# Odd experts choose their body by a row of conditional blocks, with prefetch hints for the skips at the head of each body

## The chip, the cores and the metric

One core of a Trainium2 chip runs one program. The metric is device time in microseconds (us): the median of the runs, beside one execution that the hardware profiler recorded. TensorE is called PE, VectorE DVE, ScalarE ACT and SyncE SP; SP issues the DMAs.

## What is computed

A two-layer trunk over 256 latent and 256 context tokens of width 1024. Layer 0 is a convolution and gating mixer with a dense SwiGLU. Layer 1 is a latent attention followed by a top-2-of-8 expert SwiGLU, and the change lies in the experts:

```python
def _moe(h, router, w1, w3, w2):
    ...
    logits = (hf @ router).astype(jnp.float32)
    top_v, top_i = lax.top_k(logits, TOP_K)             # TOP_K = 2 of 8
    top_w = jax.nn.softmax(top_v, axis=-1)
    gates = jnp.sum(jax.nn.one_hot(top_i, N_EXPERTS, dtype=jnp.float32) * top_w[..., None], axis=-2).astype(h.dtype)
    for e in range(N_EXPERTS):                           # D_EXPERT = 3584
        y = y + gates[:, e:e + 1] * _swiglu(hf, w1[e], w3[e], w2[e])
```

## The kernel before

Everything ahead of the experts is straight code. The router's result says how many of the 256 tokens chose each expert. The program rounds that up to groups of 32 tokens and packs, for all eight experts, a two-bit class into one integer `packed` (`class_of`, L1094). Class 0 means one group, 1 two groups, 2 three groups, 3 four groups. Each engine loads `packed` into a register (L1330) and branches on it by itself.

`expert(e, s)` (L1183) is the body of expert `e` for `s` groups. It streams the expert's weights, 42 pieces of 1 MB, through a ring of 21 rooms in SBUF; SP issues the load of a later piece as soon as PE has given a room back (`ring.load`, L172). In the body, `up` (L1198) multiplies by the first two weight matrices, `turn` (L1214) transposes, `down` (L1227) multiplies by the third, `spread` (L1253) and `scatter` (L1274) put the result back to its tokens, and DVE adds it to the stream (L1278). All f32 matmuls of `up`, `down` and `scatter` become four PE instructions each, two weight loads and two matmuls. Ahead of every even expert `gather` (L1128) collects the tokens of two experts.

For each expert four bodies stand in the program, for three, one, four and two groups, and one of them runs. Before the change they are nested else-branches (L1349 to L1358): the outermost condition is `groups != 2`, and the body for three groups is its Else. A block that ends with its Else lies last, so in the program's layout the order is one, four, two, three groups, and then the code that follows, which is called the join here. Whoever leaves the body for one, four or two groups jumps over the rest to the join; whoever leaves the body for three groups is there.

`tc.mark_branch_hint_location` puts a BRANCH_PREFETCH_HINT for a named branch into PE's program: it tells PE's instruction fetch where that branch will probably go. Without an expression it says that the branch jumps away from the block that follows it; with an expression a register decides. Before the change the named branches are the outermost ones alone, one for each expert. The order of PE, ACT and DVE is written out by hand (`ordered()`, L1109).

In the profiled execution the experts 0 to 7 have 3, 1, 4, 3, 3, 1, 3 and 3 groups.

Of the kernel before, what the change touches and what calls it, by code (L numbers as in the profile page):

```python
# [33 lines left out]
N_EXP = 8  # L34
# [210 lines left out]
def trunk(ctx: ExitStack, tc, w, out, taps=None):  # L245
# [19 lines left out]
    def scratch(dtype=F32):  # L265
        return tmp.tile([P, T], dtype, tag="tmp", name="scratch")
# [230 lines left out]
    with tc.tile_pool(name="mix", bufs=1, side="right", reuse_waits="tile") as mix:  # L497
# [163 lines left out]
        for m in range(4):  # L661
# [6 lines left out]
            s = scratch()  # L668
# [81 lines left out]
    with tc.tile_pool(name="ffn", bufs=1, side="right", reuse_waits="tile") as fp:  # L750
# [12 lines left out]
        for t in range(3):  # L763
            f0, f1 = FF_CUT[t], FF_CUT[t + 1]
            f = f0
            if t == 0:
# [5 lines left out]
                f = 2  # L772
            for f in range(f, f1):
                a1 = one(f"f1_{f}", hi, lo, T)
                a3 = one(f"f3_{f}", hi, lo, T)
                s = act(f - f0, a1, a3)
# [201 lines left out]
    more = right.enter_context(tc.tile_pool(name="more", bufs=1, side="right", reuse_waits="tile"))  # L978
# [52 lines left out]
    As, Bs = [bank("A") for _ in range(4)], [bank("B") for _ in range(2)]  # L1031
# [24 lines left out]
    other = lg.unsqueeze(2).to_broadcast([P, 2, N_EXP, N_EXP])  # L1056
# [52 lines left out]
    def ordered():  # L1109
        return tc.manual_schedule(engines={mybir.EngineType.PE, mybir.EngineType.Activation, mybir.EngineType.DVE})  # L1110

    with tc.tile_pool(name="exp", bufs=1, side="right", reuse_waits="tile") as ep:
# [219 lines left out]

        fg_row = xf_all[:, :, 0, :]

        def announce(e):
            tc.mark_branch_hint_location(f"groups{e}", hint=(packed // 4**e) % 4 != 2, engines={mybir.EngineType.PE})

        for e in range(N_EXP):
            groups = (packed // 4**e) % 4
            state = ring.loaded, ring.used  # L1340

            def body(s):
                ring.loaded, ring.used = state
                with ordered():
                    if e % 2 == 0:
                        announce(e + 1)
                    expert(e, s)

            with tc.If(groups != 2, preferred_fallthrough_block=True, label=f"groups{e}") as other:  # L1349
                with tc.If(groups == 0, preferred_fallthrough_block=True) as one:  # L1350
                    body(1)
                with one.Else():
                    with tc.If(groups == 3, preferred_fallthrough_block=True) as four:
                        body(4)
                    with four.Else():
                        body(2)
            with other.Else():
                body(3)  # L1358
            if e % 2 and e + 1 < N_EXP:
                with ordered():  # L1360
                    announce(e + 1)
                    gather([Bs[0], As[0], Bs[1], As[1]] * 2)
        assert ring.used == len(ring.pieces) == ring.loaded
        with ordered():
            final_norm()
# [196 lines left out]
```

## Time and profile before

| what | value |
|---|---|
| median of 3 runs | 1695.11 us (1694.89 to 1697.21) |
| the profiled execution's own time | 1693.19 us |
| its span, from the first to the last instruction | 1691.40 us |
| PE busy | 1606.8 us, 95% of the span |
| mean granted clock of PE | 0.982 |
| chain of work that ended last | PE 88%, DMA 6%, DVE 4% |
| PE, idle at the join behind expert 1 / inside expert 2's choice | 5.00 / 5.37 us |
| PE, idle at the join behind expert 2 / behind expert 5 | 8.17 / 5.18 us |

The experts take the last 930 us of the span. The granted clock is the share of PE's full 2.4 GHz that was granted in a stretch: 1.0 or 0.5 (1.2 GHz). In the views, "issue" as the end of an idle time says that the engine waited for nothing that the profile shows as work. PEq and PEldq are PE's sequencer, which reads instructions some time before they run; a COMPARE_BRANCH there is a branch, and its duration is the time until the next instruction could be read. Queue q8 of the DMA carries PE's instructions.

### The profile page before, as it was taken

What the parts mean: (1) busy time and instruction counts of PE and PEld (TensorE: products, weight loads), DVE (VectorE), ACT (ScalarE), POOL (GpSimd) and SP (SyncE); (2) the same over time, 40 slices, a digit from 0 to 9 for tenths busy, and PEclk for the clock granted to TensorE, in tenths of its full rate; (3) what the DMA queues carried; (4) which work ended last, traced back from release to release, by engine and by line L of the source; (5) the groups of instructions that cost most, each with busy time, mean ns of one, the idle gap of its engine ahead of it and who ended that gap; (6) DMA issues with size and microseconds to landing.
All of it is one profiled execution on the core that took longest, in us unless ns stands there. A gap on an engine that the chain in (4) does not pass through costs nothing.

```text
span 1691.4 us, 40719 instructions
## 1 busy us (share of the span) xinstructions
PE 1606.8 (95%) x18697; PEld 1100.3 (65%) x18697; DVE 518.3 (31%) x945; ACT 381.6 (23%) x708; POOL 23.1 (1%) x20
## 2 busy tenths in 40 slices
PE   8998999999999999999997699979999996999996
PEld 5776678888888877796553455545565552656554
DVE  4899773333333567751010100010010011001001
ACT  4353452222222355542000000000010010000101
POOL 0013000000000000000000000000000000000000
PEclk9999999999999999999999799989999997999999
DMA  9661663322322355599999999869989999999970
GB/s 383 234 246 54 248 246 100 100 87 95 101 90 84 103 196 209 200 370 383 398 380 420 417 417 387 297 215 383 389 311 382 392 395 419 417 418 418 418 287 28
DMA packets 67322, 470.23 MB, mean 278 GB/s; under 512 B 7456, under 2 KB 7840, under 8 KB 13088
## 3 DMA queue, kind: packets, MB, share of 16 engines
q1 hardware_dynamic: 67104, 467.13, 70.7%
q8 instruction: 160, 2.62, 0.6%
q14 instruction: 58, 0.48, 0.1%
HBM read 466.05 MB, written 1.05 MB: 276 GB/s over the span
## 4 chain that ended last, share of the span: by engine, by line
PE 88%; DMA 6%; DVE 4%; issue 1%; ACT 1%; SPq 0%; DVEq 0%; ACTq 0%
PE bankA L1198 29%; PE bankB L1227 14%; PE bankA L270 7%; PE bankA L271 7%; PE bankA L272 7%; DMA raw<-e 5%; PE bankB L271 3%; PE bankB L270 3%; PE bankB L272 3%; DVE cv L525 2%; PE bankC L340 2%; PE bankC L1214 1%; PE bankA L1274 1%; DMA room<-e 1%; PE bankA L340 1%
## 5 line engine op out<-in xcount | busy, mean ns | idle before, releaser
L1198 PE MATMUL bankA<-room,xf_all 128*32 128x256 f32 x4704 | 265.9, 384 | 14.4 <-issue 8.5
L1208 DVE TENSOR_TENSOR scratch<-scratch,bankA 128x256 f32<-128x256 f32 (+1 forms) x98 | 31.6, 352 | 721.8 <-ACT scratch L1207 721.8
L1198 PEld LDWEIGHTS bankA<-room,xf_all 128*32 128x32 f32 x4704 | 154.3, 111 | 116.4 <-issue 23.2
L1198 PE MATMUL bankA<-raw,xf_all 128*32 128x256 f32 x3024 | 171.6, 382 | 7.4 <-DMA raw<-e 7.3
L132 DVE TENSOR_TENSOR split<-raw,split 128x1024 fp32r<-128x1024 f32 (+4 forms) x121 | 139.9, 1159 | 113.4 <-ACT split L131 111.2
L131 ACT CAST split<-raw 128x1024 fp32r<-128x1024 f32 (+4 forms) x121 | 118.1, 981 | 199.4 <-PE bankA L272 121.2
L1207 ACT ACTIVATE scratch<-bankA 128x256 f32<-128x256 f32 (+1 forms) x98 | 32.5, 331 | 546.5 <-PE bankA L1198 542.8
L270 PE MATMUL bankA<-hq,split 128*128 128x512 f32 (+1 forms) x380 | 149.3, 393 | 1.3 <-ACT hq L451 1.3
L271 PE MATMUL bankA<-hq,split 128*128 128x512 f32 (+1 forms) x380 | 148.2, 390 | 0.9 <-DVE hq L454 0.9
L1227 PE MATMUL bankB<-raw,scratch 128*32 128x256 f32 x2352 | 138.6, 386 | 8.4 <-DMA raw<-e 7.9
L272 PE MATMUL bankA<-hq,split 128*128 128x512 f32 (+1 forms) x380 | 146.4, 385 | 0.0
L1198 PEld LDWEIGHTS bankA<-raw,xf_all 128*32 128x32 f32 x3024 | 96.6, 110 | 74.1 <-DMA raw<-e 9.6
L1227 PEld LDWEIGHTS bankB<-raw,scratch 128*32 128x32 f32 x2352 | 75.9, 111 | 64.0 <-DMA raw<-e 9.4
L1198 PE MATMUL bankA<-roomsplit,xf_all 128*32 128x256 f32 x1680 | 96.3, 384 | 6.0 <-DMA roomsplit<-e 6.0
L525 DVE SCALAR_TENSOR_TENSOR cv<-pad,prm,cv 128x512 f32<-128x512 f32 x106 | 86.0, 848 | 0.8
L270 PEld LDWEIGHTS bankA<-hq,split 128*128 128x128 f32 x380 | 71.6, 189 | 21.9 <-ACT hq L451 3.4
L1198 PEld LDWEIGHTS bankA<-roomsplit,xf_all 128*32 128x32 f32 x1680 | 53.6, 111 | 45.4 <-DMA roomsplit<-e 9.7
L271 PEld LDWEIGHTS bankA<-hq,split 128*128 128x128 f32 x380 | 71.7, 189 | 15.6 <-DVE hq L454 1.4
L272 PEld LDWEIGHTS bankA<-hq,split 128*128 128x128 f32 x380 | 71.5, 188 | 15.4 <-DVE split L132 0.2
L1216 ACT COPY scratch<-bankC 128x384 f32<-128x384 f32 (+2 forms) x56 | 24.6, 440 | 234.3 <-PE bankC L1214 234.3
L1227 PE MATMUL bankB<-room,scratch 128*32 128x256 f32 x1344 | 76.9, 379 | 0.0
L271 PE MATMUL bankB<-hq,split 128*128 128x512 f32 (+1 forms) x172 | 66.9, 389 | 1.4 <-DVE hq L276 1.4
(409 smaller groups left out, 2011.6 us busy)
## 6 DMA issues: line engine op xcount, KB each, us to landing
room<-e SPq DMA_DIRECT2D x144, 1024.0 KB, 10.9
raw<-e SPq DMA_DIRECT2D x125, 1024.0 KB, 12.1
roomsplit<-e SPq DMA_DIRECT2D x63, 1024.0 KB, 14.7
raw<-ada SPq DMA_DIRECT2D x48, 1024.0 KB, 7.9
raw<-f SPq DMA_DIRECT2D x26, 1024.0 KB, 5.1
raw<-f SPq DMA_DIRECT2D x8, 896.0 KB, 4.7
raw<-win SPq DMA_DIRECT2D x6, 1024.0 KB, 8.2
raw<-wout SPq DMA_DIRECT2D x4, 1024.0 KB, 8.3
```

Of the source, the lines that this page charges most:

```text
L131: self.nc.scalar.copy(wh[:, :size], raw)
L132: self.nc.vector.tensor_sub(wl[:, :size], raw, wh[:, :size].bitcast(F32))
L270: nc.tensor.matmul(acc, wh, ah, start=first, stop=False)
L271: nc.tensor.matmul(acc, wh, al, start=False, stop=False)
L272: nc.tensor.matmul(acc, wl, ah, start=False, stop=last)
L340: nc.tensor.matmul(acc[32 * q : 32 * q + 32, :], cs[:, 4 * h + q, :], wt[:, q, :], start=(h == 0), stop=(h == 1), tile_position=(0, 32 * q))
L525: nc.vector.scalar_tensor_tensor(out=o, in0=i, scalar=cw[:, m, j : j + 1], in1=o, op0=ALU.mult, op1=ALU.add)
L1198: nc.tensor.matmul(accs[g // 2][32 * q : 32 * q + 32, g % 2], xf[:, k, g * GROUP : (g + 1) * GROUP], piece[:, k - kk, :, q * P : (q + 1) * ...
L1207: nc.scalar.activation(part, acc[:, :n, 0, :], AF.Silu)
L1208: nc.vector.tensor_mul(part, part, acc[:, :n, 1, :])
L1216: nc.scalar.copy(ht[:, : s * P], tp[:, : s * P])
L1227: nc.tensor.matmul(ys[g // 2][32 * t : 32 * t + 32, g % 2], ht[:, g * P + f * GROUP : g * P + (f + 1) * GROUP], piece[:, f - ff, t, :], st ...
```

## The change

Even experts keep the nested else-branches. For odd experts each body gets a conditional block of its own, one behind the other, in the order three, one, four, two groups, so that there is nothing to jump over from else to else, but whoever leaves a body comes to a condition that is false and skips the rest. At the head of each odd body but the last stands a hint, without an expression, for the skip that follows this body. At the head of each even body stands a hint with an expression for the first branch of the odd expert that follows. Behind an odd expert, ahead of `gather`, two hints are written: for the even expert's outermost branch, as before, and for its branch to the one-group body, which is new.

```diff
-        def announce(e):
-            tc.mark_branch_hint_location(f"groups{e}", hint=(packed // 4**e) % 4 != 2, engines={mybir.EngineType.PE})
+        def hint(label, expr=None):
+            tc.mark_branch_hint_location(label, hint=expr, engines={mybir.EngineType.PE})
+
+        def case(cond, label=None):
+            return tc.If(cond, preferred_fallthrough_block=True, label=label)
 
         for e in range(N_EXP):
             groups = (packed // 4**e) % 4
+            after = (packed // 4 ** (e + 1)) % 4
             state = ring.loaded, ring.used
-
-            def body(s):
+            enter = f"three{e + 1}", after == 2
+
+            def body(s, leave):
                 ring.loaded, ring.used = state
                 with ordered():
-                    if e % 2 == 0:
-                        announce(e + 1)
+                    if leave:
+                        hint(*leave)
                     expert(e, s)
...
+            if e % 2:
+                with case(groups == 2, f"three{e}"):
+                    body(3, [f"other{e}"])
+                with case(groups != 2, f"other{e}"):
+                    with case(groups == 0):
+                        body(1, [f"more{e}"])
+                    with case(groups != 0, f"more{e}"):
+                        with case(groups == 3):
+                            body(4, [f"two{e}"])
+                        with case(groups != 3, f"two{e}"):
+                            body(2, None)
+                if e + 1 < N_EXP:
+                    with ordered():
+                        hint(f"one{e + 1}", (packed // 4 ** (e + 1)) % 2 == 0)
+                        hint(f"groups{e + 1}", after != 2)
+                        gather([Bs[0], As[0], Bs[1], As[1]] * 2)
+            else:
+                with case(groups != 2, f"groups{e}") as other:
+                    with case(groups == 0, f"one{e}") as one:
+                        body(1, enter)
+                    with one.Else():
+                        with case(groups == 3) as four:
+                            body(4, enter)
+                        with four.Else():
+                            body(2, enter)
+                with other.Else():
+                    body(3, enter)
```

Three places in PE's program, as built. The first is the join behind expert 0, where expert 1 begins. In the rows, `L1336 ISA` and `REGISTER_ALU` work out a hint's register, `room` and `raw` are rooms of the ring and `xf_all` is the gathered tokens. Before:

```order
L1349 UNCONDITIONAL_BRANCH
L1336 ISA
L1336 REGISTER_ALU
L1557 BRANCH_PREFETCH_HINT
L1349 REGISTER_ALU x2
L1349 COMPARE_AND_BRANCH
L1350 REGISTER_ALU x2
L1350 COMPARE_AND_BRANCH
L1198 MATMUL bankA<-room_5422,xf_all 32x256 x8
```

After:

```order
L1372 UNCONDITIONAL_BRANCH
L1356 REGISTER_ALU x2
L1356 COMPARE_AND_BRANCH
L1576 BRANCH_PREFETCH_HINT
L1198 MATMUL bankA<-room_5422,xf_all 32x256 x24
```

The hint that stood here (it is that of expert 2's outermost branch, put here by the scheduler, one expert ahead of its branch) is gone, and the three-group body (x24) follows the first branch, with the hint for its own exit at its head.

The second place is the end of expert 1's one-group body. Before, it ends with a jump to the join, and the next condition follows:

```order
L1274 MATMUL bankA<-scratch 128x256
L1274 MATMUL bankC<-scratch 128x256
L1350 UNCONDITIONAL_BRANCH
L1353 REGISTER_ALU x2
L1353 COMPARE_AND_BRANCH
```

After:

```order
L1359 UNCONDITIONAL_BRANCH x2
L1361 COMPARE_AND_BRANCH
L1362 REGISTER_ALU x2
L1362 COMPARE_AND_BRANCH
L1576 BRANCH_PREFETCH_HINT
L1198 MATMUL bankA<-room_5422,xf_all 32x256 x32
```

The jump to the join has become the conditional branch of L1361, to which a hint at the body's head belongs.

The third place is the join behind expert 1, ahead of the gather (`G_all`, `tok_h`) for the experts 2 and 3. Before:

```order
L1274 MATMUL bankA<-scratch 128x256
L1274 MATMUL bankC<-scratch 128x256
L1349 UNCONDITIONAL_BRANCH
L1128 MATMUL bankB<-G_all,tok_h 128x256 x2
L1128 MATMUL bankB<-G_all,tok_l 128x256 x2
```

After:

```order
L1364 UNCONDITIONAL_BRANCH x2
L1361 UNCONDITIONAL_BRANCH
L1358 UNCONDITIONAL_BRANCH
L1336 ISA
L1336 REGISTER_ALU
L1576 BRANCH_PREFETCH_HINT
L1128 MATMUL bankB<-G_all,tok_h 128x256 x2
```

One hint now stands directly ahead of the gather, and it belongs to the outermost branch of the even expert behind that gather. The second hint that the source writes there, for the branch to the one-group body, is not in the built program. The same holds behind the experts 3 and 5.

## Rows read from the trace of the kernel before

**Rows 1.** The page: span, and the DMA queue of instructions (packets, MB, share).

```profile
span 1691.4 us, 40719 instructions
...
q8 instruction: 160, 2.62, 0.6%
```

**Rows 2.** PE's timeline at joins: start us, us, what, count, [idle before, what ended it].

```profile
947.64 0.80 PE L1128 MATMUL bankB<-G_all,tok_h 128*128 128x256 f32 x2 [5.00 <-issue]
...
959.44 6.82 PE L1198 MATMUL bankA<-room,xf_all 128*32 128x256 f32 x88 [5.37 <-DMA room<-e]
...
1125.15 11.04 PE L1198 MATMUL bankA<-room,xf_all 128*32 128x256 f32 x152 [8.17 <-issue]
...
1427.12 0.48 PE L1274 MATMUL bankA<-scratch 32*128 32x256 f32 x2 [0.64 <-DVE scratch L1263]
...
1433.44 0.80 PE L1128 MATMUL bankB<-G_all,tok_h 128*128 128x256 f32 x2 [5.18 <-issue]
...
1439.73 6.63 PE L1198 MATMUL bankA<-room,xf_all 128*32 128x256 f32 x117 [0.34 <-issue]
```

**Rows 3.** Branches and hints of PE's sequencer by line: count, ns min/median/max, first and last.

```profile
L1349 PEldq COMPARE_BRANCH  x8: 73/434/2666, 760.5 to 1555.9; - x8
...
L1350 PEldq COMPARE_BRANCH  x5: 66/5960/6192, 881.0 to 1427.2; - x5
...
L1353 PEldq COMPARE_BRANCH  x2: 66/3134/6201, 958.8 to 1115.5; - x2
...
L1431 PEldq COMPARE_BRANCH  x1: 3355/3355/3355, 1676.9 to 1676.9; - x1
...
L1557 PEldq BRANCH_PREFETCH_HINT  x8: 32/38/55, 0.8 to 1439.5; - x8
...
L1349 PEldq COMPARE_BRANCH  x1: 460/460/460, 1248.9 to 1248.9; - x1
...
L1349 PEldq COMPARE_BRANCH  x1: 1239/1239/1239, 1438.0 to 1438.0; - x1
...
L1349 PEldq COMPARE_BRANCH  x1: 777/777/777, 1555.9 to 1555.9; - x1
```

**Rows 4.** Stretches: their us, PE busy (count), granted clock, DMA share, GB/s.

```profile
881.00:942.00 61.00, 45.48 (x701) 0.94 1.01 415
947.60:954.10 6.50, 6.43 (x32) 0.58 1.01 413
959.40:963.30 3.90, 3.86 (x40) 0.50 1.02 422
1125.10:1130.60 5.50, 5.45 (x52) 0.51 0.03 6
1245.20:1249.90 4.70, 4.24 (x36) 1.00 0.35 145
1367.00:1428.00 61.00, 48.50 (x713) 0.89 1.00 412
1433.40:1439.50 6.10, 5.96 (x32) 0.65 1.00 412
```

**Rows 5.** Timeline of PE's weight loads at the start of expert 4's body.

```profile
1249.90 2.31 PEld L1198 LDWEIGHTS bankA<-room,xf_all 128*32 128x32 f32 x47
1252.59 0.37 PEld L1198 LDWEIGHTS bankA<-room,xf_all 128*32 128x32 f32 x12 [0.38 <-issue]
```

**Rows 6.** Instruction fetches in DMA view: 975 to 1046 us, and 1550 to 1557 us.

```profile
q8 instruction: 10, 0.16, 0.9%
...
q8 instruction: 1, 0.02, 0.9%
```

**Rows 7.** SP's timeline of DMA issues at the change from expert 0 to 1.

```profile
876.04 2.94 SPq L172 DMA_DIRECT2D raw<-e  x2
882.60 1.14 SPq L172 DMA_DIRECT2D room<-e  x2
```

More of the change, by code (lines that the diff above doesn't have):

```diff
@@ L1340, in trunk @@
             state = ring.loaded, ring.used
-            def body(s):
+            enter = f"three{e + 1}", after == 2
+            def body(s, leave):
                 ring.loaded, ring.used = state
                 with ordered():
-                    if e % 2 == 0:
-                        announce(e + 1)
+                    if leave:
+                        hint(*leave)
                     expert(e, s)
[L1349 to L1362, printed above, removed]
+            if e % 2:
[25 more added lines that the diff above has]
+                    body(3, enter)
```

## The prediction

> **What bounds the kernel now.** I read the page first: a span of 1691.4 us [rows 1], PE busy for 95% of it. PE's idle time is therefore what such a change can give back, and in the experts I looked for it in PE's timeline. Four idle times of 5 us and more stand out, all at places where a body is left or chosen: 5.00, 5.37, 8.17 and 5.18 us [rows 2]. The sequencer's rows say what they are. The branches that no hint belongs to and that jump took 5.96 to 6.20 us each (four of those at L1350 and L1353) [rows 3]; the one behind expert 1, at about 6.0, left PE idle for 5.00, so about 1.0 us of a branch is hidden by what PE still has in its queue. The hinted branches that jump took 0.46, 0.78 and 1.24 us, the last of them with 0.34 us of idle behind it [rows 2, 3]; those that fall through take under 0.1 us. The 8.17 us are two branches in a row, 6.20 us out of expert 2's four-group body and 2.67 us into expert 3's three-group body.
>
> What a jump waits for is instruction fetch. The queue of instructions moved 160 packets of 2.62 MB in all, 16 KB each [rows 1], and in 71 us of steady work 10 of them [rows 6], one per 7.1 us. From the counts of the built program that is one block of 256 PE instructions, at 28 ns each. After a hinted jump into expert 4's body, 47 weight loads with their matmuls and three instructions ahead of them ran, 97 instructions, and then PE stood still for 0.38 us [rows 5]: the block in which the jump had landed was at its end, and the next one not yet there. So the next block is asked for when a block is entered. And although the hint for the jump at 1555.9 us was executed at 1439.5 us, the one fetch ahead of it comes in the last 7 us [rows 3, 6]: the hint changes which block is asked for when the block with the branch is entered. A block takes about 3.4 us when the weights' DMA rests (3.36 us at L1431) and 6.0 us when it runs at full rate [rows 3].
>
> Two more things bound what follows. After an idle time of 5 us the granted clock is 0.5 for some microseconds: the gather behind expert 1 took 6.5 us at a mean of 0.58, that behind expert 3 took 4.7 us at 1.00, and the first 3.9 us of expert 2 and 5.5 us of expert 3 ran at 0.50 and 0.51 [rows 4]. And experts 1 and 5, with one group, are bound by the weights: PE busy 45 to 49 of 61 us, DMA at 412 to 415 GB/s, its ceiling here [rows 4]. A wait of PE inside them costs nothing, unless it delays the first rooms that they give back.
>
> **The change part by part.** All in us, against the profiled execution; times are those of before.
>
> *Leaving expert 1.* The unhinted jump becomes a branch whose hint stands at the head of the body, 60 us ahead. Counting instructions from the place of [rows 5] through the built order, the branch lies some 175 instructions behind the start of its block, more than 6 us at the end of this body, so the target is there. Idle 5.00 falls to 0.3 (the next register instructions), and the gather runs at full clock, 4.7 instead of 6.4: −6.4. The DMA is at its ceiling across this join, 1.05 MB in 2.5 us, and expert 2 takes 42 such pieces in 157 us, 3.7 each (959.44 to the 8.17 us ahead of 1125.15) [rows 2, 4], so the weights don't take the gain back.
>
> *Inside expert 2.* The hint for the branch to the one-group body is not in the built program. The jump over that body stays unhinted: 5.37 remains, 0.
>
> *Expert 2 to 3.* The jump out of the four-group body stays unhinted, but the three-group body of expert 3 now follows the join directly: the branch of 2.67 and the hint's 0.25 ahead of it go, 8.17 becomes 5.25. The stretch at half clock should shorten as behind the other gaps, from 5.5 to about 3.9, which is worth half the difference: together −3.5.
>
> *Expert 3 to 4.* Where the three-group body fell through to the join, it now skips three bodies, hinted 120 us ahead and 240 instructions into its block: hidden, as the 0.46 and 0.78 were. But the hint for the next jump, into expert 4's three-group body, now stands only one gather ahead of it, executed just after its own block was entered. I take it that a hint acts then too: the target needs 3.4, the gather covers 3.6 of sequencer time. That target starts about 24 instructions before the end of a block (before: 97). The next block comes 3.4 after the jump; 24 instructions (0.7) and the queue (about 0.8) cover part: 1.9 of idle, of which before paid 0.3. +1.6.
>
> *Into experts 1 and 5.* Instead of falling through, PE skips the three-group body, hinted. For expert 5 the branch lies 80 instructions into its block, 2.2, so some 1.2 of its 3.4 remain visible in part; the first rooms come back later by about 0.4 and 0.6, and these experts, DMA-bound, pass that on: +1.0. SP makes the same skip without a hint, over 88 instructions. But SP has issued its last load of expert 0 by 878.98 and waits until 882.60 for PE's first room [rows 7]: 3.6 in hand, against at most 6.0 for a fetch. I take 0 here, and up to 2.4 at each of the two experts in the range.
>
> *Expert 5 to 6.* The branch out of the one-group body lies only 57 instructions into its block, and that is entered when the last piece is there: about 1.8 ahead of the branch, of which 0.64 are the wait for DVE [rows 2]. Of 6.0 at full DMA rate, 4.2 remain, less 1.0 hidden: 5.18 becomes 3.1. The gather gets perhaps 0.5 of its lost clock back [rows 4]. The late hint again: the jump to expert 6's body shows 0.5 instead of 0.34. That target starts about 82 instructions (2.3) before a block's end, against some 190 before: 6.0 − 2.3 − 0.4 = 3.3 of idle. Sum −2.1 − 0.5 + 0.2 + 3.3 = +0.9.
>
> *Expert 6 to 7.* A jump and a 0.5 stop in the block behind it become a fall-through: −0.5. Behind expert 7 all engines skip three bodies. PE is done by then; for ACT and DVE these are under 150 instructions, and I take 0, with 3 at the end of the range.
>
> Sum: −6.4 − 3.5 + 1.6 + 1.0 + 0.9 − 0.5 = −6.9. The profiled execution, 1693.2 with 1691.4 of span, would become 1686.3; the median of the runs stands 1.9 above it, so 1695.1 − 6.9 = **1688.2**.
>
> **The rivals.** *The late hint does nothing.* Every hint of before stood a whole body or more ahead of its branch, in the body ahead or, by the scheduler, at the join ahead of that; none was executed inside the branch's own block after that had been entered. If it is too late there, the jump into expert 4 shows 3.4 − 1.0 and the block behind it 2.8 (4.9 instead of 1.6), and that into expert 6 shows 5.0 instead of 0.5: +7.9, 1696.1, no change that can be measured.
>
> *The block ends lie elsewhere.* My instruction counts decide three costs, and some ten instructions that the loader moves would shift them. If targets start early in their blocks and expert 5's branch late, 1.6 and 3.3 go and leaving expert 5 gives as much as leaving expert 1: about −16, 1679.
>
> *The hints don't cover the new skips: slower.* The place is the odd experts' joins. The Trainium skill, "Runtime: NRT & Kernel Launch", section "Instruction fetch mechanics", says that a taken branch whose target is outside the small window of resident blocks forces a fetch before execution goes on. By that rule alone every new skip stalls, and the change adds three ahead of the last. The unhinted branches of the trace agree (5.96 to 6.20), the hinted ones do not (0.46 to 1.24) [rows 3]. In rows: nothing gained behind experts 1 and 5, −3.5 at expert 3, +2.4 leaving expert 3, +2.4 each into experts 1 and 5, +4.9 and +8.4 at experts 4 and 6: +17, 1712. It decides if a hinted skip costs more than some 3 us on average. Against it: the first hint of the program, without an expression like the new ones, belongs to the jump into expert 0, which took 0.41 (with the 0.46 it makes the median of 0.434 at L1349) [rows 3].
>
> **How the numbers follow.** My forecast 0.43, late hint without effect 0.32, block ends elsewhere 0.15, hints not covering 0.10. A measurement of this kernel tells about 0.2%, 3.4 us, from no change. Below 1691.7 lie most of the forecast (0.37), the third case and a little of the second (0.03): faster 0.55. Above 1698.5 lie the last case and 0.02 of the second: slower 0.12. The rest, 0.33, is the same. For 8 in 10 the range runs from 1680, where most of the third case ends, to 1698, the second case with SP's skips.
>
> **What would show it.** Right: idle behind expert 1 under 1 us and that gather at clock 1.0; 5.4 still inside expert 2; 5 to 5.5 ahead of expert 3; twelve hints executed. The late hints: the branches of L1372 behind the gathers of experts 3 and 5 take under 1.5 us, or 3 to 6. The block ends: PE stops of 2 to 3 us some 24 and 82 instructions into the bodies of experts 4 and 6, and a branch of about 4 us out of expert 5. Wrong: a branch of 6 us at L1356, L1358 or L1361, or experts 1 or 5 longer than 61 us.

## The result: 90 us slower, most of it in two waits of 40 us

| what | before | after |
|---|---|---|
| median | 1695.51 us (4 runs, 1694.89 to 1697.21) | 1785.13 us (4 runs, 1782.30 to 1787.87) |
| ratio of the times, 95% interval | | 1.0524 [1.0512, 1.0537] |
| span of the profiled execution | 1691.40 us | 1781.49 us |
| mean granted clock of PE | 0.982 | 0.955 |

The prediction, 1688.2 with a range of 1680 to 1698, was wrong in sign and by 97 us.

From the page of after, against [rows 1]: PE runs the same 18697 matmuls, its share fell from 95% to 91%, and only two more blocks of PE's instructions were fetched.

```profile
span 1781.5 us, 40908 instructions
...
PE 1617.8 (91%) x18697; PEld 1107.0 (62%) x18697; DVE 518.5 (29%) x945; ACT 383.7 (22%) x710; POOL 23.1 (1%) x20
...
q8 instruction: 162, 2.65, 0.6%
```

PE's timeline of after at the same joins as [rows 2] (start us, us, operation, count, idle time before it and what ended it):

```profile
887.70 2.79 PE L1198 MATMUL bankA<-room,xf_all 128*32 128x256 f32 x24 [4.26 <-SPq L1356]
...
953.36 0.80 PE L1128 MATMUL bankB<-G_all,tok_h 128*128 128x256 f32 x2 [2.58 <-DVEq L1361]
...
999.66 10.60 PE L1198 MATMUL bankA<-room,xf_all 128*32 128x256 f32 x160 [39.78 <-SPq L1361]
...
1162.38 7.92 PE L1198 MATMUL bankA<-room,xf_all 128*32 128x256 f32 x100 [5.28 <-issue]
...
1287.57 0.79 PE L1128 MATMUL bankB<-G_all,tok_h 128*128 128x256 f32 x2 [5.37 <-PEq L1358]
...
1414.78 1.50 PE L1198 MATMUL bankA<-room,xf_all 128*32 128x256 f32 x22 [2.70 <-DVEq L1356]
...
1478.42 0.79 PE L1128 MATMUL bankB<-G_all,tok_h 128*128 128x256 f32 x2 [2.58 <-DVEq L1361]
...
1526.19 4.13 PE L1198 MATMUL bankA<-room,xf_all 128*32 128x256 f32 x48 [40.98 <-SPq L1361]
```

The releasers tell the story. Before, the idle times ended with "issue" or a piece's DMA. Now the first matmul of expert 2 and of expert 6 waits about 40 us for SP at L1361, the condition behind the one-group body, and four others end with DVE or SP at such a condition. Put together from this timeline, place by place (after minus before, us):

| place | difference |
|---|---|
| ahead of the experts | +2.0 |
| entering expert 1; its body; leaving it; gather | +4.3; +1.9; -2.4; +0.1 |
| ahead of expert 2 | **+34.4** |
| expert 2 to 3; bodies of 2 and 3 | -2.9; -0.4 |
| leaving expert 3, gather, entering 4 | +7.7 |
| body of 4; entering 5; its body; leaving it; gather | -0.2; +2.7; +0.4; -2.6; +0.8 |
| ahead of expert 6 | **+40.7** |
| bodies of 6 and 7 | +1.1 |
| from PE's last matmul to the end | +2.6 |
| sum | +90.2 (spans: +90.1) |

What SP did at L1361 behind expert 1 (one line of the kernel: operations, ns, first and last start; then who waited), and the first two rows of the same behind expert 5:

```profile
L1361 SPq EVENT_SEMAPHORE  x8: 17/17/17, 989.6 to 999.6; - x8
L1361 SPq COMPARE_BRANCH  x2: 43/46/50, 980.2 to 999.7; - x2
...
who waited for it (us, times):
  PE bankA L1198: 39.8, 1
```
```profile
L1361 SPq EVENT_SEMAPHORE  x8: 17/17/17, 1525.6 to 1526.1; - x8
L1361 SPq COMPARE_BRANCH  x2: 38/44/50, 1506.1 to 1526.2; - x2
```

SP's timeline of DMA issues behind expert 1, to be read against [rows 7]:

```profile
974.65 5.31 SPq L172 DMA_DIRECT2D raw<-e  x3
1005.14 3.78 SPq L172 DMA_DIRECT2D room<-e  x2
```

SP came to the condition at 980.2, took the branch at once, and then spent 19.5 us on eight semaphore instructions. Each is a wait with an addition. The first five start 16 or 17 ns behind the landing of SP's last load on the same semaphore, among them these four: landings at 991.975, 994.458, 996.950, 999.389; instructions at 991.992, 994.475, 996.967, 999.405. On the other three semaphores the last load had landed by 987.0, and their instructions follow by 999.6. Behind expert 5 it is the same wait: SP came at 1506.1, and the first of the eight waited for the last load, which landed at 1525.56. So of each long wait 20 to 21 us passed before SP came (PE was ready at 959.9 and 1485.2), and about 20 after that. I call this **booking**: whoever skips a block must leave each semaphore as if the block had run, so SP adds what the block's loads would have added, and first waits until its own loads on that semaphore have landed. That this is what the additions are for is my reading of the built program. The Trainium skill, "DMA: Bandwidth & Descriptors", section "Why a DMA increments its semaphore by 16 and not by 1", says what is at stake: a count tells of landed data only when it is complete. No run here shows what would happen without the wait.

In the built program the false way out of each block of a row carries these waits on SP. The one behind L1359 looks like this, and that behind L1361 is built alike. With else-branches there are none, and the trace of before has no such addition on SP in the experts; I put it down to one of the bodies always running, and all four loading the same number of pieces.

```
L1359 UNCONDITIONAL_BRANCH
L1359 UNCONDITIONAL_BRANCH [waits DMAHW0_49,DMAHW1_49,DMAHW2_49,DMAHW3_49,DMAHW4_49,DMAHW5_49,DMAHW6_49,DMAHW7_49]
L1361 COMPARE_AND_BRANCH
```

PE's side of it is expert 2's first matmul, as built before and after (its four bodies wait for the same semaphores):

```
L1198 MATMUL bankA<-room_5422,xf_all 32x256 [waits DMAHW6_49,DVE_49]
L1198 MATMUL bankA<-room_5422,xf_all 32x256 [waits DMAHW2_49,DMAHW4_49,DMAHW0_49,DMAHW6_49,DVE_49]
```

Its room may have been filled in any of four blocks, which are no longer alternatives, so it waits for four DMA semaphores instead of one, and three of the counts come from bookings. The mean clock of 0.955 is for the most part no cause: while PE stood still from 959.9 to 999.6, 0.53 was granted (first row: its us; busy us and count of PE, PEld, DVE, ACT and POOL; granted clock, DMA share, GB/s), and that enters the mean. What is a cause is the second row: the gather behind expert 3, which ran at 1.00 before [rows 4], now at 0.56; it took 1.9 us more.

```profile
959.90:999.60 39.70, 0.00 (x0) 0.00 (x0) 0.48 (x1) 0.03 (x1) 0.00 (x0) 0.53 0.96 397
...
1287.50:1294.30 6.80, 6.65 (x32) 6.46 (x32) 1.49 (x4) 1.89 (x4) 0.00 (x0) 0.56 0.03 7
```

### The profile page after: what moved, and what is told of

The parts are those of the page before. It is cut to its first block, busy times and chain, and to the rows that moved or that the text cites. A ratio compares the mean times of both kernels' runs of the same rounds, so it can differ in the third digit from the quotient of the medians.

```text
span 1781.5 us, 40908 instructions
## 1 busy us (share of the span) xinstructions
PE 1617.8 (91%) x18697; PEld 1107.0 (62%) x18697; DVE 518.5 (29%) x945; ACT 383.7 (22%) x710; POOL 23.1 (1%) x20
## 5 line engine op out<-in xcount | busy, mean ns | idle before, releaser
L272 PEld LDWEIGHTS bankA<-hq,split 128*128 128x128 f32 x380 | 71.6, 188 | 15.2 <-DVE split L132 0.5
```

The costliest lines, as they stand in the source:

```text
L272: nc.tensor.matmul(acc, wl, ah, start=False, stop=last)
```

## The experiments

The theories were: **A**, SP's booking, as read above; **B**, instruction fetch, on which the prediction was built; **C**, a fixed price for every condition passed. A had to be put in a second form, A2, on the way. A time without a ratio comes from one run; the kernel before lay between 1691.6 and 1698.5 us in all its runs here.

### Without the hints

```diff
                 with ordered():
-                    if leave:
-                        hint(*leave)
                     expert(e, s)
...
-                        hint(f"one{e + 1}", (packed // 4 ** (e + 1)) % 2 == 0)
```

> The changed kernel with its rows of blocks, without the hints for the odd experts' skips; only the hint for the even expert's outermost branch stays, ahead of the gather. Theory A (booking of the loads): in the trace of the changed kernel SP, when it skips a body, waits in turn for eight DMA semaphores, and each wait ends 17 ns after the last load on that semaphore has landed (991.975 to 991.992, 999.389 to 999.405); PE's first piece waits for the counts that SP adds only then. That has nothing to do with the hints: both idle times of 39.8 and 41.0 us ahead of experts 2 and 6 stand again, and the skips without hints (6 us each, entering experts 1 and 5) lie beside SP's waits of 4.3 and 2.7 or cost up to 3 us more. 1785 to 1791. Theory B (instruction fetch, the one my prediction was built on): the loss comes from hints that send the fetch to the wrong block. Without them the two long idle times go and every skip costs its 6 us: about 1705 to 1720.

Measured: 1798.6, beside 1698.0 for the kernel before on that chip, and 8 us above the range that A gave. Both long waits stood (38.4 and 34.9 us, the second with a longer jump ahead of it). B falls as the cause of the loss; with the hints it is some 11 us smaller (89.6 instead of 100.6). The scheduler also moved the three hints that stayed to 762 us, far from their branches, so a part of the 11 belongs to that.

### A block that is never entered, in the kernel before

```diff
+            if e == 1:
+                with tc.If(packed > 4**N_EXP - 1):
+                    for i in range(8):
+                        nc.sync.dma_start(spare[:, i * 8 : i * 8 + 8], w["prm"][:, i * 8 : i * 8 + 8])
```

> The kernel before, with one more conditional block behind expert 1, ahead of the gather. Its condition is never true; it holds eight loads of 4 KB into a spare tile, one on each DMA semaphore. Theory A: SP comes to the block at 979 us of the trace of before (5.1 us of it the far jump at 974.1), waits for the last loads on the eight semaphores, the last of which lands at 993.5, and adds to them; PE, which began expert 2 at 959.4, has to wait with its first piece until about 994. +34.5: 1727 to 1732. Theory B: a block of some ten instructions is skipped inside a fetched stretch of the program, 0 to 1 us: 1695 to 1698. Theory C (every condition passed costs the engines a meeting of fixed length, wherever it stands): the same cost here as behind expert 3; with the changed kernel's 40 us shared by two skips, about 20.

> The same block behind expert 1 with one load of 4 KB instead of eight. Theory A: SP adds to one semaphore alone, that of the fifth load from the end of expert 1, which lands at about 983.6; expert 2's first piece was loaded on that same semaphore, so PE waits until then instead of beginning at 959.4. +24: 1717 to 1722, and between the kernel before and the block with eight loads. Theory B: 0 to 1 us, 1695 to 1698. Theory C: the same as with eight loads.

> The block with eight loads behind expert 3 instead of expert 1. Expert 3 has three groups and is bound by PE: in the trace of before SP issues its last load there at 1242.5, it lands at 1248.9, and PE begins expert 4 at 1249.9. Theory A: SP's wait for the landing takes the place of its far jump of 5.2 us, and the counts are there before PE asks: 0 to 1 us, 1695 to 1698. Theory B: the same. Theory C: the same as behind expert 1, 1715 or more.

Measured: 1694.7, 1695.6, 1696.8. These three missed their place: nothing tied the block to expert 1 or 3, and the scheduler put it ahead of expert 0, where SP passed it at 759 to 762 us. They still show the booking alone: with eight loads behind expert 1 SP was held for 11 us (761.3 to 772.5), with one for 0.2, and neither moved the time beyond the scatter.

So the loads were tied to the place by their source, the stream that the expert has just written:

```diff
+                        nc.sync.dma_start(spare[:, i * 8 : i * 8 + 8], xt[:, 0, i * 8 : i * 8 + 8])
```

> The kernel before with a never-true conditional block behind expert 1, which stands there now: its eight loads of 4 KB read the stream that expert 1 has just written, so that it can't be moved ahead of the experts, as the same block with loads from a constant was. Theory A (booking): SP comes to it at about 979 us of the trace of before, waits until the last of its loads on each of the eight semaphores has landed (993.5), adds, and PE, whose first piece of expert 2 came on one of the last of these semaphores, begins at about 994 instead of 959.4. +34.5: 1728 to 1733. Theory B (fetch): 0 to 1 us. Theory C (every condition costs a meeting of the engines): the same for four loads, for one load and behind expert 3.

> The same with four loads. Theory A: SP adds to four semaphores, those of the loads that land at 976.1, 978.6, 981.1 and 983.6. Expert 2's first piece came on the last of the four, so PE begins at about 983.8 instead of 959.4. +24: 1718 to 1722. Theory B: 0 to 1. Theory C: as with eight loads.

> The same with one load. Theory A: SP adds to one semaphore, whose last load landed at 976.1, before SP comes at 979.2, so SP does not wait; PE asks for that semaphore first for expert 2's sixth piece, at 979.9. 0 to 1 us: 1695 to 1698. Theory B: 0 to 1. Theory C: as with eight loads.

> Eight loads, behind expert 3, which has three groups and is bound by PE. SP issues its last load there at 1242.5, it lands at 1248.9, and PE begins expert 4 at 1249.9. Theory A: the wait lasts until 1248.9 and takes the place of SP's far jump of 5.2 us: 0 to 1 us, 1695 to 1698. Theory B: the same. Theory C: as behind expert 1.

Measured: 1695.5, 1700.4, 1696.1, 1696.8, beside 1696.5. SP's line and PE's timeline with eight loads behind expert 1:

```profile
L1361 SPq EVENT_SEMAPHORE  x8: 17/17/17, 988.4 to 993.6; - x8
L1361 SPq COMPARE_BRANCH  x1: 50/50/50, 978.5 to 978.5; - x1
...
who waited for it (us, times):
busy tenths in 40 slices 0000000000000000000000000000000000000000
```
```profile
959.80 15.66 PE L1198 MATMUL bankA<-room,xf_all 128*32 128x256 f32 x256 [5.84 <-DMA room<-e]
```

SP was held from 978.5 to 993.6 as expected, and PE began expert 2 at 959.8 all the same. A, in the form that SP's wait costs the time, falls, and C with it. (The 4 us of the run with four loads come from a single run, and nothing in its trace waits for L1361; I leave them open.) Expert 2's first matmul still waits for one DMA semaphore in the kernel with eight loads, at the count that its own load gave, which comes before anything that SP adds. That gave A2: what costs is that **PE's piece could have come from the skipped block**. The same block, with its loads into the rooms that expert 2 reads first:

```diff
+                        nc.sync.dma_start(ring.rooms[(ring.used + i) % len(ring.rooms)][:, :8], w["prm"][:, :8])
```

> The never-true block behind expert 1 of the kernel before again, but its eight loads now go into the first eight rooms from which expert 2 will read. Theory A2 (booking, second form): with loads into a spare tile SP waited for the landings (978.5 to 993.6) and PE did not care. What PE waits for are the semaphores of every load that may have filled the room it reads; if one of them stands in a skipped block, its count comes from SP's booking alone, at the end of the skip. In the program PE's first matmul of expert 2 now waits for two DMA semaphores instead of one. SP books at 993.3, PE begins there instead of at 959.4 to 960.8: +33: 1726 to 1732. Theory A (SP's wait alone) has fallen with the spare tile: 1695 to 1698 if it were all. Theory C: a fixed cost, the same as with one load.

> The same with one load, into the first room of expert 2. Theory A2: the one semaphore is that whose last load has landed by 976.1, so SP does not wait for it; but SP itself comes to the block only at 979 to 980, because it issues the loads of expert 1 at the rate at which they land and is some 20 us behind PE there. PE begins expert 2 at about 980.4: +20: 1713 to 1718. So the two parts of the 34 us are told apart: 20 until SP comes, 13 for the landings. Theory C: as with eight loads.

Measured: 1729.3 and 1717.0, beside 1695.1: +34 and +22. Eight loads (SP's line, then PE's timeline), then one load in the same way:

```profile
L1360 SPq EVENT_SEMAPHORE  x8: 17/17/17, 988.4 to 993.7; - x8
...
who waited for it (us, times):
  PE bankA L1198: 38.5, 1
```
```profile
993.53 6.81 PE L1198 MATMUL bankA<-room,xf_all 128*32 128x256 f32 x88 [38.50 <-SPq L1360]
```
```profile
L1360 SPq EVENT_SEMAPHORE  x1: 17/17/17, 981.0 to 981.0; - x1
...
who waited for it (us, times):
  PE bankA L1198: 25.6, 1
```
```profile
981.14 15.60 PE L1198 MATMUL bankA<-room,xf_all 128*32 128x256 f32 x256 [25.64 <-SPq L1360]
```

This settles it for the wait ahead of expert 2. SP's eight instructions are the same as with the spare tile, at the same times to 0.1 us; what differs is the row "who waited for it", empty there, PE here. And the cost falls into two parts. PE waited 5.4 us there before; the one load made that 25.6, and these 20 us are SP's way to the condition: in an expert bound by the weights it issues one load for each that lands, 19.8 us ahead of its landing (979.63 and 999.39 in after), and so comes to the join when PE has long left it. The other seven made it 38.5, and these 13 are the landings. The wait ahead of expert 6 had no such experiment of its own; it shows the same rows, and the next two runs place it.

### Where the loss sits

The rows for two of the four odd experts, the others nested as before:

```diff
+            row = (1, 5)
...
-            if e % 2:
+            if e in row:
                 with case(groups == 2, f"three{e}"):
```

> The changed kernel's rows of blocks for experts 1 and 5 alone; experts 3 and 7 are nested as before. Read from the two traces, what the change costs there: entering expert 1 +4.3, its body +1.9, its exit -2.4, the wait ahead of expert 2 +34.4; entering expert 5 +2.7, its body +0.4, its exit -2.6, the gather +0.8, the wait ahead of expert 6 +40.7. Theory A2 (booking): +80, 1775, and 1770 to 1779. If the cost came from every row alike, half of the 90: 1740.

> The rows for experts 3 and 7 alone, which have three groups and are bound by PE. Theory A2: SP has its last load out 5 us before PE is done and books while PE gathers, so no long wait stands; what is left are jumps: expert 2 to 3 -2.9, leaving expert 3 and the gather behind it +7.7, the end of the program +2.6: +7, 1702, range 1697 to 1707. With the other half the sum is the whole change. If every row costs alike: 1740.

Measured: 1779.6 for experts 1 and 5, +84; 1708.5 for 3 and 7, ratio 1.0070 [1.0054, 1.0085], +13. The loss belongs to the one-group experts, as A2 has it, and "every row alike" falls. Both lie just above the ranges that I gave (+80 and +7 were expected). In the second, PE's timeline shows why:

```profile
1123.84 13.03 PE L1198 MATMUL bankA<-room,xf_all 128*32 128x256 f32 x192 [5.33 <-issue]
...
1246.47 0.50 PE L1128 MATMUL bankB<-G_all,tok_h 128*128 128x256 f32 x2 [2.65 <-DVEq L1359]
...
1254.08 6.25 PE L1198 MATMUL bankA<-room,xf_all 128*32 128x256 f32 x75 [3.61 <-issue]
```

The jumps into experts 4 and 6 took 3.9 and 6.1 us, and nothing hides them here. For expert 4 the hint stands directly ahead of the gather, 5 us before the jump. For expert 6 the scheduler had put it at the join behind expert 4, as in the kernel before, and it ran at 1372.6, 74 us before the jump:

```profile
L1368 PEldq COMPARE_BRANCH  x1: 6112/6112/6112, 1446.2 to 1446.2; - x1
```

So this jump is slow with an early hint too; that the hint comes late is not shown to be the reason in the changed kernel either (6.17 there). In the whole change this jump, worth 5.5 us of idle time, lies under the wait of 41 us, which is most of the 7 us by which the halves together exceed the whole.

### The order of the blocks

```diff
-            enter = f"three{e + 1}", after == 2
+            enter = f"three{e + 1}", after != 3
...
-                with case(groups == 2, f"three{e}"):
-                    body(3, [f"other{e}"])
+                with case(groups == 3, f"three{e}"):
+                    body(4, [f"other{e}"])
...
-                            body(2, None)
+                            body(1, None)
```

> The changed kernel with the blocks of the odd experts in another order: four, two, three, one groups, so that behind the one-group body no block is left to skip. Theory A2: ahead of experts 2 and 6 there is nothing to book, the idle times of 39.8 and 41.0 us fall to what the inner branch costs (5.4 ahead of expert 2, up to 6 ahead of expert 6). Behind expert 1 and 5 PE stands 0.3 instead of 5. Entering experts 1 and 5 SP books three blocks and waits for its last landing as now (some 6.5 us, 4 to 5.5 of them visible at PE). Experts 3 and 7 cost more: one of their two skips at the entry has no hint (6), and one block is skipped behind them. Against the kernel before: -6.4 +4.5 +4 +3 +1.3 +4.5 -6 +2.5 +11 = +18, 1713, range 1705 to 1725. If the cost belonged to the rows of blocks as such, or to the hints: 1780 or more, since experts 1 and 5 skip as many blocks as before.

Measured: 1775.1, ratio 1.0473 [1.0456, 1.0491], against 1713 expected, 50 us above the range. PE's waits in the experts (us in total, times, longest), and its timeline ahead of experts 2 and 6:

```profile
PE bankA L1198 <- PEq L1362: 30.9, 2, 15.7
PE bankA L1198 <- SPq L1359: 28.9, 1, 28.9
PE bankA L1198 <- PEq L1359: 15.6, 1, 15.6
```
```profile
971.46 8.90 PE L1198 MATMUL bankA<-room,xf_all 128*32 128x256 f32 x125 [6.38 <-issue]
...
1484.66 4.45 PE L1198 MATMUL bankA<-room,xf_all 128*32 128x256 f32 x34 [5.86 <-DMA room<-e]
```

The part that A2 spoke of came true: with nothing to skip behind the one-group body, 39.8 and 41.0 became 6.4 and 5.9. But the loss came back at the entries: 15.2, 15.6, 15.7 and 28.9 us ahead of experts 1, 3, 5 and 7. Two of the causes are mine. The hint for the first skip had its condition the wrong way round (`after != 3` for a block on `groups == 3`), and those four jumps took 4.6 to 6.8 us; and I had priced one fetch for an entry, where each further block skipped without a hint fetches again (4.2 to 6.6 us each). Of the 28.9 the first 13.5 are such jumps, and the rest is the booking once more: SP books the first block ahead of expert 7 at 1628.2 to 1633.4, PE being ready at 1619.4.

### Else-branches and another body last

Nothing is booked if all bodies are alternatives. In the first kernel the body that falls through to the join is the one-group body for odd experts; in the second, which knows the input, each expert's own:

```diff
-            with tc.If(groups != 2, preferred_fallthrough_block=True, label=f"groups{e}") as other:
+            with tc.If(groups != last, preferred_fallthrough_block=True, label=f"groups{e}") as other:
...
             with other.Else():
-                body(3)
+                body(last + 1)
```

> The kernel before, with nested else-branches everywhere, but for odd experts the outermost Else, which falls through to the join, is the one-group body instead of the three-group body (three, four, two groups are nested ahead of it). All bodies are alternatives, so nothing is booked (A2): no wait of SP for landings, and PE's waits are those of before. Leaving experts 1 and 5 loses its jump (-6.4 and -5.7), expert 3 is entered by falling through (8.17 becomes 5.3 and its half clock shortens: -4.5), leaving expert 3 gets an unhinted jump (+6), entering experts 1 and 5 a hinted one (+0.5). Sum -10: 1685, range 1681 to 1690. Theory B of instruction fetch gives the same here; what it tests is that the fetch part of the prediction was sound where no load is booked.

> Not a kernel to keep, since it was written with the classes of this input known: nested else-branches in which for each expert the body that will run is the outermost Else. It is reached by one hinted jump over the three others and falls through to the join; nothing is booked. The rows of before give 5.00, 5.37, 8.17 and 5.18 us of idle time to be had, and about 4 more from the stretches at half clock; entering experts 1 and 5 costs a hinted jump, 0.4 to 5 us each. -22: 1673, range 1668 to 1681. If the unhinted jumps are not what PE waits for at these places, 1690 or more.

Measured: 1693.4, ratio 0.9990 [0.9980, 0.9999], a tenth of a per cent, and above the range of 1681 to 1690; and 1674.2, 0.9873 [0.9858, 0.9888], as expected. The second says that the idle times of [rows 2] were what the prediction took them for: without the unhinted jumps 21 us go. In both the jump into expert 5 is slow although its hint was executed 117 us earlier (branch of one_else there; then own_last's eight outermost branches, ns min/median/max):

```profile
L1354 PEldq COMPARE_BRANCH  x1: 5106/5106/5106, 1366.6 to 1366.6; - x1
```
```profile
L1354 PEldq COMPARE_BRANCH  x8: 352/420/5471, 761.3 to 1537.0; - x8
```

One hinted jump in eight was not covered. In the first kernel it cost 4.3 us of idle time and 2.0 in the body behind it, most of what is missing to the 10 us expected; the way from expert 2 to 3 gave 2.0 instead of 4.5. No kernel written without knowledge of the input beat the one before by more than that; with it 1.3% can be had, about the 24 us of idle time at the joins [rows 2].

### Which hints act

One more hint for each even expert, to the inner branch, at the heads of the bodies ahead of it; the hint for the outermost branch moves there too, from the join just ahead of these bodies:

```diff
+                    if e % 2 and e + 1 < N_EXP:
+                        tc.mark_branch_hint_location(f"one{e + 1}", hint=(packed // 4 ** (e + 1)) % 2 == 0, engines={mybir.EngineType.PE})
                     expert(e, s)
```

> The kernel before, nested, with one more hint for each even expert: for its inner branch, to or past the one-group body. Both hints of an even expert stand at the heads of the bodies of the odd expert ahead of it. Theory H1 (each hint belongs to its branch): the inner branch of expert 2, 5.96 us without a hint, takes under 1.5, the jumps into experts 4 and 6 keep their 0.46 and 1.24: -5 to -6, 1689 to 1691. Theory H2 (a later hint takes the place of an earlier one): the inner hint puts out the outer one for experts 4 and 6, whose jumps then take 3.4 to 6: -5 +3 +5 = +3, 1696 to 1700.

Measured: 1704.9, ratio 1.0052 [1.0038, 1.0066], slower than either theory had it. The inner branch of expert 2, then the outer ones of experts 4 and 6:

```profile
L1352 PEldq COMPARE_BRANCH  x1: 877/877/877, 953.2 to 953.2; - x1
```
```profile
L1351 PEldq COMPARE_BRANCH  x1: 3422/3422/3422, 1242.5 to 1242.5; - x1
```
```profile
L1351 PEldq COMPARE_BRANCH  x1: 6226/6226/6226, 1439.0 to 1439.0; - x1
```

The new hint did its work (0.88 for 5.96), and the two jumps that it was not meant for lost theirs (0.46 and 1.24 before [rows 3]). That speaks for H2, a later hint puts out an earlier one; but these two jumps' own hints had moved as well, and the code by a few instructions. The last two runs put each hint into the middle of the body ahead of its branch, so that none stands between a hint and its branch:

```diff
                 if j == 1:
+                    if e + 1 < N_EXP:
+                        announce(e + 1)
```

> The kernel with the one-group body as the outermost Else of the odd experts (1693.4 before), with every hint executed in the middle of the body that runs ahead of its branch, so that no other hint is executed between a hint and its branch. Theory H2 (a later hint puts out an earlier one): the jump into expert 5 falls from 5.1 us to under 1.5, the others stay under 1.3: -4, 1689, range 1686 to 1691. Theory H3 (the place of the branch in its fetched block decides): the jump into expert 5 keeps 4 to 5.5 us, since the instructions stand where they stood within three: 1693, range 1691 to 1695.

> The same shift of the hints in the kernel in which each expert's own body falls through (1674.2). H2: the jump into expert 5 from 5.47 to under 1.5: 1670, range 1667 to 1672. H3: unchanged, 1674, range 1672 to 1676.

Measured: 1697.7, ratio 1.0012 [1.0003, 1.0021], and 1680.7, 0.9920 [0.9902, 0.9937]; both lie above the ranges of H2 and of H3. The jumps into experts 5 and 6 in the first (in the second they took 5.43 and 3.93 us):

```profile
L1354 PEldq COMPARE_BRANCH  x1: 5481/5481/5481, 1365.2 to 1365.2; - x1
```
```profile
L1354 PEldq COMPARE_BRANCH  x1: 3581/3581/3581, 1438.2 to 1438.2; - x1
```

The jump into expert 5 stayed, so no later hint was putting it out; H2 is not its cause. H3 (the place in the fetched block) kept that jump right but did not foresee that the one into expert 6 rose from 0.37 to 3.6 with code moved by a few instructions. Which hinted jump is covered stays **open**: these runs show that it is neither the time between hint and branch alone (57 to 119 us for jumps of 0.35 to 0.46 us, 56 to 117 us for jumps of 3.6 to 5.5) nor a hint in between alone.

## Why the prediction was wrong, point by point

**The step that failed** is the one on SP in "Into experts 1 and 5": "SP makes the same skip without a hint ... I take 0 here, and up to 2.4 at each". It priced a skip as a branch, for PE and for SP, and let instruction fetch be all that a skip can cost. The skip on SP is eight waits for landings, each with an addition that PE's next piece waits for. The step on leaving expert 1 had no SP in it at all. The rows that could have said so were at hand: the built program names the waits on each false way out, and the trace of before shows SP issuing its last load of expert 1 at 973.7, 14 us after PE had begun expert 2. The worst case that I had, 1712, was again fetch alone. The term that was missing is +34.4 and +40.7.

- **Leaving expert 1** (-6.4): -2.3 with the gather. The branch was hidden as said, 0.34 us where 6.0 stood, but the idle time is 2.58, not 0.3: DVE books too, after its last addition to the stream, and the gather waits for that. The gather still ran at a granted clock of 0.57 and took 6.5 us, not 4.7.
- **Inside expert 2** (0): the branch took its 6.17 us, under the long wait.
- **Expert 2 to 3** (-3.5): right, 5.28 us idle against 5.25 predicted, -2.9; of the clock's 0.8 us 0.3 came. (With these terms the sum was -3.7, not -3.5.)
- **Expert 3 to 4** (+1.6): +7.7. The hinted skip of three bodies, which I had put 240 instructions into its block, took 5.63 us, as much as in the kernel without hints (5.28); the gather behind it, at 0.56, took 2 us more. The jump into expert 4 behind the late hint took 1.69, so the hint acted in part, and the stop 24 instructions into expert 4 did not come.
- **Into experts 1 and 5** (+1.0): +4.3 and +2.7 of idle time, and +2.3 in the bodies. Into expert 1 it is SP's booking, not the branch (0.47). Into expert 5 the branch took 2.29, more than I had left visible (1.2); together with the conditions behind it, it held PE for 2.1, and DVE's booking, which ended the wait, added 0.5.
- **Expert 5 to 6** (+0.9): idle time 2.58 (I had 3.1, and by its terms 3.2), but that is luck: the branch out of the body took 1.77, not the 4.2 that I had counted, and what PE waited for is again DVE's booking. The jump into expert 6 took 6.17, under the long wait.
- **Expert 6 to 7** (-0.5): right, no stop is left there.
- **The end** (0, up to 3): +2.6, but not for the skip that I had in mind. ACT loads its function tables twice more:

```profile
1768.47 1.28 ACT L1311 ACT_TABLE_LOAD   x1 [8.66 <-DVEq L1358]
...
1770.93 1.28 ACT L1313 ACT_TABLE_LOAD   x1
```

They stand in the tail of every kernel here that has a row of blocks for expert 7, and in no other; I take it that behind a body that may or may not have run the program loads its table again. 2 x 1.28 is the whole difference. The Trainium skill, "ScalarE: Activation LUTs", section "What ACT_TABLE_LOAD costs", has 1283 ns for one, and so has this trace.

The branches of PE in after that carry the points above:

```profile
L1356 PEldq COMPARE_BRANCH  x1: 467/467/467, 882.2 to 882.2; - x1
```
```profile
L1356 PEldq COMPARE_BRANCH  x1: 2289/2289/2289, 1410.8 to 1410.8; - x1
```
```profile
L1361 PEldq COMPARE_BRANCH  x1: 342/342/342, 950.0 to 950.0; - x1
```
```profile
L1361 PEldq COMPARE_BRANCH  x1: 1768/1768/1768, 1475.1 to 1475.1; - x1
```
```profile
L1373 PEldq COMPARE_BRANCH  x1: 6166/6166/6166, 958.3 to 958.3; - x1
```
```profile
L1358 PEldq COMPARE_BRANCH  x1: 5629/5629/5629, 1281.3 to 1281.3; - x1
```
```profile
L1372 PEldq COMPARE_BRANCH  x1: 1694/1694/1694, 1292.1 to 1292.1; - x1
```
```profile
L1372 PEldq COMPARE_BRANCH  x1: 6167/6167/6167, 1483.0 to 1483.0; - x1
```

Of the rivals, "the late hint does nothing" gave the right time for the jump into expert 6 and was half right for expert 4, though for expert 6 its reason is not shown (an early hint did no better in the rows for experts 3 and 7); "the hints don't cover the new skips" was right for one skip of three (5.63) and in part for a second (2.29). The signs that the prediction had named for being wrong came (5.63 at L1358, and expert 1 at 63.1 us instead of 61), but none of them points at SP. All this was small beside what was not on the list. The counting of places in blocks held for the branch out of expert 1, and not for those out of 3 and 5, nor for the stop in expert 4. And one reading of [rows 3] was too kind to the hints: all eight outermost branches of before have one, so the 2.67 us into expert 3 were a hinted jump too, beside the 0.46 to 1.24 that the prediction names. The rule of the Trainium skill, "Runtime: NRT & Kernel Launch", section "Instruction fetch mechanics", that a taken branch out of the resident window waits for a fetch, is borne out by the unhinted jumps over a body in the kernel without hints (5.3 to 7.3 us from expert 1 to expert 6), and not by the hinted ones of 0.34 to 0.47.

## What to carry to other kernels

Before a chain of alternatives is turned into a row of conditional blocks, read on every engine what the way around a block does: a block that issues DMAs leaves waits for landings behind on the issuing engine, and a consumer of a buffer that the block might have filled then waits for that engine. The price is the lag of the issuing engine behind the consumer, and the landings on top: here 34 to 41 us behind experts bound by the DMA, and 0 to 4.3 us where PE was the bottleneck in the changed kernel. And a gain of a few microseconds from branch hints has to be measured in the final layout, because moving a hint, or a few instructions, can take it away at another branch.

## What was not expected of the hardware

- A wait that nobody waits for is free: SP held for 15.1 us (978.5 to 993.6) cost nothing measurable with a spare tile; with the rooms as targets the same eight instructions made the kernel 34 us slower.
- A hint moves a jump from about 6 us to 0.34 to 0.88 at best, but in the kernel before, and in each kernel above whose branches are shown, at least one hinted jump still took over 2 us, up to 6.2.
